# TensorE reads its moving operands from two halves in turn, with the evacuations in the matching order

## Chip, core and metric

The kernel runs on one core of a Trainium2 chip. The metric is the device time of one execution in microseconds; a run's time is the median of its executions. The profile is of one execution, taken by the hardware profiler.

## What is computed

One layer of a hybrid decoder on 512 tokens of 1,024 channels, all in float32. Cut to what matters here:

```python
h = rms_norm(x, g_mix_pre)
z = h @ w_in                                   # 1024 -> 4608: pool, rnn x, rnn gate, two merge gates
y_pool = pool_mixer(z_pool) @ w_pool_out       # causal means over 2, 4, 8, 16 tokens, small maps
y_rnn = rg_lru_branch(z_x, z_g) @ w_rg_out     # causal conv over 4 tokens, gates, linear recurrence, GELU
merged = sigmoid(z_gp) * y_pool + sigmoid(z_gr) * y_rnn
x = x + rms_norm(merged @ w_o, g_mix_post)
h = rms_norm(x, g_ffn_pre)
up = h @ w_up                                  # 1024 -> 6144
hid = gelu(causal_conv3(up[:, :3072])) * up[:, 3072:]
x = x + rms_norm(hid @ w_down, g_ffn_post)     # 3072 -> 1024
x = x + sigmoid(rms_norm(x, g_ple_gate) @ w_ple_gate) * rms_norm(p @ w_ple_proj, g_ple_post)
```

## The kernel before

Every float32 matrix is split into a high part rounded to the float32r type and a low part, the rest. A product is then three float32r matmuls into one PSUM bank, which `mm3` issues: high by high, high by low, low by high (lines 198, 199 and 200 of the profile; nearly all TensorE work carries these line numbers). ScalarE makes the high part (a copy with rounding, L412 and L193), VectorE the low one (a subtraction, `sub`, L189). Weights come from memory through `raw` tiles, and `weight(key)` keeps a few of them prepared ahead in a fixed order.

The stages, in the order in which TensorE runs them (its order is written out by hand; the other engines' order is made by a scheduler, with raised priorities where the code says `urgent`):

1. The input projection. The first four tiles (`rx`, L503) go over all channels while everything is loaded. `in_tile` makes each later tile of 128 output channels: weights stationary, the normalised transposed tokens `ht` (tag A, 512 columns) moving. `scaled` (L562) takes a tile out of its bank and multiplies it by the tokens' inverse norms `rb`. The recurrent gates (`gates`, L606) are pairs of 64-row matmuls. `pool_map`, and the two output projections into `gate` tiles (L831, L832), follow.
2. `ple_tile` projects the per-layer embedding; the product with `w_o` (`product`, tokens stationary, weight tiles `hi`, `lo` moving, 512 columns) is made by a seven-product scheme of the Strassen-Winograd kind on half blocks.
3. `add_norm` (L850, L853) and `x2_out` normalise; `h2_tile` transposes tokens on TensorE (L858) and splits them into halves of 256 tokens (`h2h`, `h2l`, tag C).
4. The up projection, also by seven products: twelve pairs of tiles, weights stationary, token forms of 256 columns moving (`products`, `up_product`; the first pair plainly by `up_plain`). Forms 5, 6, 7 and 3 are tiles of tag A that start at column 48 of their buffers (`PLACE_UP`). Forms 1, 2 and 4 lie in tag C: 1 and 2 are the first half of the tokens at column 1,072, form 4 is the second half at column 46 (`PLACE_H2`). A pair runs the products in the order 1, 3 (of the pair before), 6, 2, 7, 5, 4. `gated_half` (L998, L1000) makes the convolution along the tokens straight from the bank, `hidden` the product with the other half.
5. The down projection, seven products again, weights moving at 512 columns, then the last normalisation, `x3_tile`, and the gate of the embedding (`w_ple_gate`, 512 columns; the very last tile in two halves of 256), with its sigmoid (L164) out of PSUM and two VectorE steps before each store (L1249, L1250).

Sums of weight blocks that the schemes need are made partly on VectorE (L348) and partly by DMAs that accumulate in memory, issued from GpSimd.

The moving operand, third argument of a matmul, is a run of neighbouring columns everywhere in this version.

Of the kernel before, what the change touches and what calls it, by code (L numbers as in the profile page):

```python
# [9 lines left out]
F32 = mybir.dt.float32  # L10
F32R = mybir.dt.float32r
AF = mybir.ActivationFunctionType
# [69 lines left out]
def block_kernel(  # L82
# [79 lines left out]
    def act(o, i, func, after=None, **kw):  # L162

        ins = ACT.activation(o, i, func, **kw)  # L164
# [26 lines left out]
    def split(hi, lo, src):  # L191

        last_copy[0] = ACT.copy(hi, src)  # L193
        sub(lo, src, hi.bitcast(F32))

    def mm3(o, a, b, start, stop, **kw):
        (ah, al), (bh, bl) = a, b
        PE.matmul(o, ah, bh, start=start, stop=False, **kw)  # L198
        PE.matmul(o, ah, bl, start=False, stop=False, **kw)  # L199
        PE.matmul(o, al, bh, start=False, stop=stop, **kw)  # L200
# [17 lines left out]
    def c1(j):  # L218
        return col[:, j : j + 1]
# [277 lines left out]
    for k in range(KD):  # L497
        w = weight(("rx", k // 2), ahead=3)
        (wh, wl), (hh, hl) = w, ht(k)
        for i, (a, b) in enumerate(((wh, hh), (wl, hh), (wh, hl))):  # L500
            for m in range(4):
                o = (k % 2) * S + m * P
                PE.matmul(rx[m], a[:, o : o + P], b, start=k == 0 and i == 0, stop=k == KD - 1 and i == 2)  # L503


    bd = quad("C").rearrange("p (s a) c -> p s (a c)", s=2)
# [52 lines left out]
        return ps  # L559

    def scaled(ps, o):
        return V.tensor_tensor(o, ps, rb, ALU.mult)  # L562

    xs, xc, xcs, sig = {}, {}, {}, {}
    r_t, a_t, rg_t = {}, {}, {}
# [31 lines left out]
    def gates(cs):  # L597

        pss = {}
        for c in cs:  # L600
            pss[c] = bank(), bank()
            hi, lo = xcs[c]
            o = slice(c * P, (c + 1) * P)
            for i, (a, b) in enumerate(((0, hi), (0, lo), (1, hi))):
                for ps, pr in zip(pss[c], HEADS):
                    PE.matmul(ps, bd[pr, a, o], b[pr], start=i == 0, stop=i == 2)  # L606
        ba, bb = HEADS
        for c in cs:
            r_t[c] = slot()
            sig[c] = temp()  # L610
            g = C_BG + c
            act(r_t[c][ba], pss[c][0][ba], AF.Sigmoid, bias=col[ba, g : g + 1])
            act(sig[c][ba], pss[c][0][bb], AF.Sigmoid, bias=bias[bb, c : c + 1])
            act(r_t[c][bb], pss[c][1][ba], AF.Sigmoid, bias=bias[ba, c : c + 1])
            act(sig[c][bb], pss[c][1][bb], AF.Sigmoid, bias=col[bb, g + KD : g + KD + 1])

    def gated(c):
        inv(V.tensor_tensor(xc[c], sig[c], xc[c], ALU.mult))
# [84 lines left out]
    def pool_map(g):  # L703
        pw = weight("pool_w")
        ps = bank()
        mm3(ps, pick(pw, g * P, (g + 1) * P), pools[g], True, True)
        hi, lo = slot(F32R), slot(F32R)
        ACT.activation(hi, ps, AF.Identity, scale=c1(C_PSCALE + g))
        V.scalar_tensor_tensor(lo, ps, c1(C_PSCALE + g), hi.bitcast(F32), ALU.mult, ALU.subtract)
        yp[g] = (hi, lo)  # L710


# [25 lines left out]
    def ple_tile(t):  # L738
        pair = []
        for h in range(2):  # L740
            w = weight(("wpp", h))
            ps = bank()
            for k in range(2):
                a = pick(pq[k], t * P, (t + 1) * P)
                mm3(ps, a, pick(w, k * S, (k + 1) * S), k == 0, k == 1)
            pair.append(ps)
        outs = [slot(), slot()]
        V.tensor_copy(outs[0], pair[0])
        ACT.copy(outs[1], pair[1])
# [66 lines left out]
    for m in range(KD):  # L816
        w = weight(("wpo", m))
        pa = bank()
        for k in range(4):
            mm3(pa, pick(w, k * P, (k + 1) * P), yp[k], k == 0, k == 3)  # L820
        w = weight(("wrg", m))
        if m == KD - 1:
            o_form(1)
        split_early(1)
        pb = bank()
        for k in range(KD):
            y = yh[k // 4][:, k % 4, :], yl[k // 4][:, k % 4, :]
            mm3(pb, pick(w, k * P, (k + 1) * P), y, k == 0, k == KD - 1)
        a, b = gate[m], gate[8 + m]
        with urgent():  # L830
            V.tensor_tensor(a, pa, a, ALU.mult)  # L831
            V.tensor_tensor(b, pb, b, ALU.mult)  # L832
            V.tensor_tensor(mq[m % 2][:, m // 2, :], a, b, ALU.add)
        if m == KD - 1:
            o_form(2)
        if m == PLE_AT:
            pled = dram.tile([S, D], F32, name="pled")
            pq = []
            for k in range(2):
                raw = temp()  # L840
                nc.sync.dma_start(raw, p_t[k])
                pq.append((slot(F32R), slot(F32R)))
                split(*pq[k], raw)

    def add_norm(pair, g, res):

        og = []
        for h in range(2):
            og.append(temp())
            V.tensor_tensor(og[h], pair[h], g[h], ALU.mult)  # L850
        r = rstd_of(pair)
        for h in range(2):
            V.scalar_tensor_tensor(res[h], og[h], r, res[h], ALU.mult, ALU.add)  # L853
# [18 lines left out]
    def h2_tile(t):  # L872
        for h in range(2):
            ps = transposed(h2n[t, h]).rearrange("p (k c) -> p k c", k=4)
            hi, lo = (v[h][t // 2][:, :, t % 2 * P : (t % 2 + 1) * P] for v in (h2h, h2l))
            with tc.high_priority(offset=2 * URGENT if t else URGENT):
                split(hi, lo, ps)
                h2_done[0] = last_copy[0].ins.name
            b, c = divmod(t, 2)
            q = 10 * b + h + 11  # L880
            if c == 0:
                h2f[q] = {k: slot() for k in (0, 2)}
            for k in (0, 2):
                ACT.copy(h2f[q][k].rearrange("p (k c) -> p k c", k=2)[:, :, c * P : (c + 1) * P], ps[:, k : k + 2, :])

# [10 lines left out]
    def products(o, w, i, form, start):  # L896
        for k in range(4):
            lhs = tuple(v[:, i, k * P : (k + 1) * P] for v in w)
            rhs = tuple(v[:, k, :] for v in form)
            mm3(o, lhs, rhs, start and k == 0, k == 3, skip_group_check=True)  # L900

    def up_plain(f, b):
        for i in range(2):
# [328 lines left out]
    for h in range(2):  # L1232
        for t in range(NT):
# [5 lines left out]
            for a, b in parts:  # L1239
                ps = bank()  # L1240
                for k in range(KD):
# [3 lines left out]
                    q = (k % 4) * P  # L1245
                    x3k = pick(x3t[t, k // 4], q, q + P)
                    mm3(ps[:, a:b], x3k, pick(w, (k % 2) * S + a, (k % 2) * S + b), k == 0, k == KD - 1)
                act(o[:, a:b], ps[:, a:b], AF.Sigmoid, scale=r3[t])
                V.tensor_tensor(o[:, a:b], o[:, a:b], ple[t // 2][:, i, a:b], ALU.mult)  # L1249
                V.tensor_tensor(o[:, a:b], o[:, a:b], x3[t // 2][:, i, a:b], ALU.add)  # L1250
                nc.sync.dma_start(out[t * P : (t + 1) * P, h * S + a : h * S + b], o[:, a:b])
# [79 lines left out]
```

## Time and profile before

| | us |
|---|---|
| median of 3 runs | 735.63 (734.74 to 736.74) |
| the profiled execution, its own time | 734.33 |
| its span | 732.6 |
| TensorE busy (4,281 matmuls) | 726.2 |
| weight loads busy | 640.3 |
| VectorE busy | 577.7 |
| ScalarE busy | 443.1 |
| GpSimd busy | 82.4 |

The span is the stretch from the first to the last instruction of the profile; the 1.7 us between it and the execution's own time lie around it. A row of a group reads: line, engine, operation, result and operand by their names and shapes, count, then busy time in us, mean ns of one, and the idle time before them with what ended it. A row of the timeline begins with the start and the length in us. A row of the windows gives a stretch's length, then for each engine its busy time and count, then the granted clock, the DMA share and GB/s. Matmuls overlap and their ends are modelled, so what one costs is read from the distance between two starts.

### The profile page before, as it was taken

The numbers are of one execution on the slowest core, as the hardware profiler recorded it, in microseconds if no ns is written. First come the engines' busy times: TensorE is split into PE (matmuls) and PEld (weight loads), VectorE is DVE, ScalarE is ACT, GpSimd is POOL, SyncE is SP. The second block draws the span as 40 slices with busy tenths as digits, with TensorE's granted clock in tenths as the row PEclk, the third lists the DMA queues.
The fourth block names the chain that finished last, engine by engine and source line by source line (L and its number), as shares of the span: only waits on it lengthen the run. The fifth ranks groups of instructions, "written<-read, shape, count | busy, mean of one in ns | idle before, by whom it ended". The sixth has DMA issues, their size and how long they took to land.

```text
span 732.6 us, 11226 instructions
## 1 busy us (share of the span) xinstructions
PE 726.2 (99%) x4281; PEld 640.3 (87%) x4281; DVE 577.7 (79%) x749; ACT 443.1 (60%) x670; POOL 82.4 (11%) x107
## 2 busy tenths in 40 slices
PE   9999999999999999999999999999999999999997
PEld 7887778888888888889999999999999888888886
DVE  4896735999646668676989999998999997789852
ACT  6746779844543344577856666666667666565721
POOL 0311212100000000111013222221200000001100
PEclk9999999999999999999999999999999999999999
DMA  8999777674788987995478999898966676767011
GB/s 325 385 310 267 166 219 186 149 210 133 257 299 275 329 316 283 313 327 206 127 270 249 270 283 266 288 239 295 237 197 224 217 238 200 261 200 271 17 58 57
DMA packets 64933, 172.53 MB, mean 236 GB/s; under 512 B 5808, under 2 KB 6448, under 8 KB 64560
## 3 DMA queue, kind: packets, MB, share of 16 engines
q1 hardware_dynamic: 50336, 129.78, 51.0%
q0 software_dynamic: 14400, 41.95, 24.6%
q8 instruction: 33, 0.54, 0.3%
q14 instruction: 20, 0.16, 0.1%
q10 hardware_dynamic: 144, 0.10, 0.0%
HBM read 155.03 MB, written 58.72 MB: 292 GB/s over the span
## 4 chain that ended last, share of the span: by engine, by line
PE 96%; DMA 2%; DVE 0%; ACT 0%; SPq 0%; POOL 0%; issue 0%; DVEq 0%
PE ps L198 31%; PE ps L200 31%; PE ps L199 31%; DMA C<-in_x_dram 1%; PE ps L858 1%; PE ps L606 1%; DMA m<-in_x_t_dram 1%; PE ps L503 1%; ACT C L486 0%; SPq L403 0%; DVE lo L189 0%; POOL s L434 0%; PE ps L548 0%; DVE t L494 0%; ACT t L164 0%
## 5 line engine op out<-in xcount | busy, mean ns | idle before, releaser
L189 DVE TENSOR_TENSOR lo<-raw,hi 128x1024 fp32r<-128x1024 f32 (+2 forms) x193 | 224.7, 1184 | 53.6 <-ACT hi L412 30.6
L198 PE MATMUL ps<-A,hi 128*128 128x256 f32 (+1 forms) x608 | 197.5, 325 | 0.0
L199 PE MATMUL ps<-A,hi 128*128 128x256 f32 (+1 forms) x608 | 197.0, 324 | 0.0
L200 PE MATMUL ps<-A,lo 128*128 128x256 f32 (+1 forms) x608 | 196.9, 324 | 0.0
L412 ACT CAST hi<-raw 128x1024 fp32r<-128x1024 f32 (+1 forms) x112 | 113.0, 1015 | 110.7 <-PE ps L199 46.6
L198 PEld LDWEIGHTS ps<-A,hi 128*128 128x128 f32 x608 | 114.2, 188 | 11.2 <-issue 0.7
L200 PEld LDWEIGHTS ps<-A,lo 128*128 128x128 f32 x608 | 114.2, 188 | 10.1
L199 PEld LDWEIGHTS ps<-A,hi 128*128 128x128 f32 x608 | 114.2, 188 | 9.8
L198 PE MATMUL ps<-C,hi 128*128 128x256 f32 (+1 forms) x392 | 116.8, 298 | 0.0
L199 PE MATMUL ps<-C,hi 128*128 128x256 f32 (+1 forms) x392 | 116.4, 297 | 0.0
L200 PE MATMUL ps<-C,lo 128*128 128x256 f32 (+1 forms) x392 | 116.4, 297 | 0.0
L193 ACT CAST hi<-raw 128x1024 fp32r<-128x1024 f32 x78 | 80.7, 1052 | 31.2 <-PE ps L199 26.4
L198 PE MATMUL ps<-hi,A 128*128 128x512 f32 x224 | 87.5, 391 | 0.0
L200 PE MATMUL ps<-hi,A 128*128 128x512 f32 x224 | 87.2, 389 | 0.0
L199 PE MATMUL ps<-lo,A 128*128 128x512 f32 x224 | 87.2, 389 | 0.0
L199 PEld LDWEIGHTS ps<-C,hi 128*128 128x128 f32 x392 | 73.8, 188 | 2.6
L198 PEld LDWEIGHTS ps<-C,hi 128*128 128x128 f32 x392 | 73.7, 188 | 2.7 <-ACT rb L441 0.2
L200 PEld LDWEIGHTS ps<-C,lo 128*128 128x128 f32 x392 | 73.7, 188 | 2.5
L434 POOL TENSOR_TENSOR s<-s,mhalf 128x1 f32<-128x1 f32 (+1 forms) x21 | 15.8, 752 | 357.8 <-DVE s L447 338.7
L200 PEld LDWEIGHTS ps<-hi,A 128*128 128x128 f32 x224 | 42.1, 188 | 8.8
L198 PEld LDWEIGHTS ps<-hi,A 128*128 128x128 f32 x224 | 42.1, 188 | 8.6
L199 PEld LDWEIGHTS ps<-lo,A 128*128 128x128 f32 x224 | 42.1, 188 | 8.5
(191 smaller groups left out, 1025.6 us busy)
## 6 DMA issues: line engine op xcount, KB each, us to landing
raw<-in_w_up_dram SPq DMA_DIRECT2D x46, 512.0 KB, 6.7
wdsum<-in_w_down_dram POOLq DMA_DIRECT2D x36, 512.0 KB, 8.5
raw<-in_w_in_dram SPq DMA_DIRECT2D x32, 512.0 KB, 7.0
raw<-wdsum SPq DMA_DIRECT2D x24, 512.0 KB, 4.4
raw<-in_w_down_dram SPq DMA_DIRECT2D x18, 512.0 KB, 3.5
wosum<-in_w_o_dram POOLq DMA_DIRECT2D x12, 512.0 KB, 9.6
wdsum<-wdsum POOLq DMA_DIRECT2D x12, 512.0 KB, 7.5
parts<-hi SPq DMA_DIRECT2D x10, 512.0 KB, 4.0
```

The costliest lines, as they stand in the source:

```text
L189: V.tensor_tensor(o, a, b, ALU.subtract)
L193: last_copy[0] = ACT.copy(hi, src)
L198: PE.matmul(o, ah, bh, start=start, stop=False, **kw)
L199: PE.matmul(o, ah, bl, start=False, stop=False, **kw)
L200: PE.matmul(o, al, bh, start=False, stop=stop, **kw)
L412: ACT.copy(hi, raw)
L434: last_pow[0] = nc.gpsimd.tensor_tensor(y, v, mhalf[:, :n], ALU.pow).ins.name
L503: PE.matmul(rx[m], a[:, o : o + P], b, start=k == 0 and i == 0, stop=k == KD - 1 and i == 2)
L606: PE.matmul(ps, bd[pr, a, o], b[pr], start=i == 0, stop=i == 2)
L858: PE.transpose(ps[:, q * P : (q + 1) * P], a[:, q * P : (q + 1) * P], ident)
```

## The change

`mm3`, the first four tiles and the gates hand TensorE the moving operand through `turns`, a view of the same columns in the order 0, n/2, 1, n/2 + 1 and so on. The result's columns come out in that order, so every step that takes such a bank out of PSUM reads it through `back` (all even columns, then all odd ones) and writes its own rows plainly (`row` cuts them into the two halves). Where such a bank is squared for a norm or copied to another bank, the order is left alone.

In the up projection the tokens have to come out in order, because the convolution runs along them. There `h2_tile` stores each block of 128 tokens as its 64 even and then its 64 odd ones (`apart` reads, `kept` writes), and `near` reads a block's two halves in turn, so that the columns come out as the tokens are. The up projection's own evacuations are not changed. Transposes are not changed.

```diff
+    def turns(a):
+        return a.rearrange("p (a b) -> p b a", a=2)
+    def back(ps):
+        return ps.rearrange("p (b a) -> p a b", a=2)
+    def row(a):
+        return a.rearrange("p (a b) -> p a b", a=2)
+    def near(v):
+        return v.rearrange("p (c a b) -> p c b a", a=2, b=P // 2)
+    def apart(v):
+        return v.rearrange("p k (b a) -> p k a b", a=2)
+    def kept(v):
+        return v.rearrange("p k (a b) -> p k a b", a=2)
-    def mm3(o, a, b, start, stop, **kw):
-        (ah, al), (bh, bl) = a, b
+    def mm3(o, a, b, start, stop, order=turns, **kw):
+        (ah, al), (bh, bl) = a, map(order, b)
...
-                PE.matmul(rx[m], a[:, o : o + P], b, start=k == 0 and i == 0, stop=k == KD - 1 and i == 2)
+                PE.matmul(rx[m], a[:, o : o + P], turns(b), start=k == 0 and i == 0, stop=k == KD - 1 and i == 2)
...
     def scaled(ps, o):
-        return V.tensor_tensor(o, ps, rb, ALU.mult)
+        return V.tensor_tensor(row(o), back(ps), row(rb), ALU.mult)
...
-                    PE.matmul(ps, bd[pr, a, o], b[pr], start=i == 0, stop=i == 2)
+                    PE.matmul(ps, bd[pr, a, o], turns(b[pr]), start=i == 0, stop=i == 2)
...
-            act(r_t[c][ba], pss[c][0][ba], AF.Sigmoid, bias=col[ba, g : g + 1])
+            act(row(r_t[c][ba]), back(pss[c][0][ba]), AF.Sigmoid, bias=col[ba, g : g + 1])
...
-            V.tensor_tensor(a, pa, a, ALU.mult)
-            V.tensor_tensor(b, pb, b, ALU.mult)
+            V.tensor_tensor(row(a), back(pa), row(a), ALU.mult)
+            V.tensor_tensor(row(b), back(pb), row(b), ALU.mult)
...
-            V.tensor_tensor(og[h], pair[h], g[h], ALU.mult)
+            V.tensor_tensor(row(og[h]), back(pair[h]), row(g[h]), ALU.mult)
...
-                split(hi, lo, ps)
+                split(kept(hi), kept(lo), apart(ps))
...
-                ACT.copy(h2f[q][k].rearrange("p (k c) -> p k c", k=2)[:, :, c * P : (c + 1) * P], ps[:, k : k + 2, :])
+                ACT.copy(kept(h2f[q][k].rearrange("p (k c) -> p k c", k=2)[:, :, c * P : (c + 1) * P]), apart(ps[:, k : k + 2, :]))
...
-            mm3(o, lhs, rhs, start and k == 0, k == 3, skip_group_check=True)
+            mm3(o, lhs, rhs, start and k == 0, k == 3, near, skip_group_check=True)
...
-                act(o[:, a:b], ps[:, a:b], AF.Sigmoid, scale=r3[t])
+                act(row(o[:, a:b]), back(ps[:, a:b]), AF.Sigmoid, scale=r3[t])
```

The same `row` and `back` stand in the other three sigmoids of the gates, in `pool_map` and in the two copies of `ple_tile`.

More of the change, by code (lines that the diff above doesn't have):

```diff
@@ L611, in gates @@
             g = C_BG + c
-            act(r_t[c][ba], pss[c][0][ba], AF.Sigmoid, bias=col[ba, g : g + 1])
-            act(sig[c][ba], pss[c][0][bb], AF.Sigmoid, bias=bias[bb, c : c + 1])
-            act(r_t[c][bb], pss[c][1][ba], AF.Sigmoid, bias=bias[ba, c : c + 1])
-            act(sig[c][bb], pss[c][1][bb], AF.Sigmoid, bias=col[bb, g + KD : g + KD + 1])
+            act(row(r_t[c][ba]), back(pss[c][0][ba]), AF.Sigmoid, bias=col[ba, g : g + 1])
+            act(row(sig[c][ba]), back(pss[c][0][bb]), AF.Sigmoid, bias=bias[bb, c : c + 1])
+            act(row(r_t[c][bb]), back(pss[c][1][ba]), AF.Sigmoid, bias=bias[ba, c : c + 1])
+            act(row(sig[c][bb]), back(pss[c][1][bb]), AF.Sigmoid, bias=col[bb, g + KD : g + KD + 1])
     def gated(c):
@@ L707, in pool_map @@
         hi, lo = slot(F32R), slot(F32R)
-        ACT.activation(hi, ps, AF.Identity, scale=c1(C_PSCALE + g))
-        V.scalar_tensor_tensor(lo, ps, c1(C_PSCALE + g), hi.bitcast(F32), ALU.mult, ALU.subtract)
+        ACT.activation(row(hi), back(ps), AF.Identity, scale=c1(C_PSCALE + g))
+        V.scalar_tensor_tensor(row(lo), back(ps), c1(C_PSCALE + g), row(hi.bitcast(F32)), ALU.mult, ALU.subtract)
         yp[g] = (hi, lo)
@@ L747, in ple_tile @@
         outs = [slot(), slot()]
-        V.tensor_copy(outs[0], pair[0])
-        ACT.copy(outs[1], pair[1])
+        V.tensor_copy(row(outs[0]), back(pair[0]))
+        ACT.copy(row(outs[1]), back(pair[1]))
         s = rstd_of(pair)
```

## Prediction

> **What bounds the kernel now.** I read the page first, then the waits of TensorE, then TensorE's groups with shapes kept apart, then its timeline at chosen places, because only start times show what a matmul costs (their ends are modelled). The page:
>
> ```profile
> span 732.6 us, 11226 instructions
> PE 726.2 (99%) x4281; PEld 640.3 (87%) x4281; DVE 577.7 (79%) x749; ACT 443.1 (60%) x670; POOL 82.4 (11%) x107
> PEclk9999999999999999999999999999999999999999
> PE 96%; DMA 2%; DVE 0%; ACT 0%; SPq 0%; POOL 0%; issue 0%; DVEq 0%
> ```
>
> TensorE is busy for 99% of the span at the full granted clock, and 96% of the chain that ended last is TensorE's. All that it waited for:
>
> ```profile
> PE ps L216 <- DVE mhalf L210: 1.1, 1, 1.1
> PE ps L503 <- ACT hi L409: 0.4, 1, 0.4
> PE ps L503 <- DVE lo L189: 0.3, 1, 0.3
> ```
>
> 1.8 us, all at the start. So the time is the sum of TensorE's steps from one matmul to the next; nothing else decides anything while that stands. How many matmuls of each shape (the rows of L199 and L200 repeat those of L198 with the same counts):
>
> ```profile
> L198 PE MATMUL ps<-A,hi 128*128 128x512 f32 x256 | 100.2, 391 | 0.0
> L198 PE MATMUL ps<-A,hi 128*128 128x256 f32 x352 | 97.3, 276 | 0.0
> L198 PE MATMUL ps<-C,hi 128*128 128x256 f32 x328 | 91.9, 280 | 0.0
> L198 PE MATMUL ps<-hi,A 128*128 128x512 f32 x224 | 87.5, 391 | 0.0
> L199 PE MATMUL ps<-C,hi 128*128 128x512 f32 x64 | 24.9, 389 | 0.0
> L198 PE MATMUL ps<-hi,h 128*128 128x512 f32 x56 | 22.0, 393 | 0.0
> L503 PE MATMUL ps<-A,hi 128*128 128x512 f32 x64 | 16.5, 394 | 0.4 <-ACT hi L409 0.4
> L199 PE MATMUL ps<-m,hi 128*128 128x512 f32 x36 | 14.0, 389 | 0.0
> L503 PE MATMUL ps<-A,lo 128*128 128x512 f32 x32 | 8.7, 394 | 0.3 <-DVE lo L189 0.3
> L606 PE MATMUL ps<-m,C 64*128 64x512 f32 x48 | 6.6, 408 | 0.0
> L198 PE MATMUL ps<-hi,m 128*128 128x512 f32 x16 | 6.3, 396 | 0.0
> L198 PE MATMUL ps<-hi,h 128*128 128x256 f32 x16 | 4.5, 283 | 0.0
> L858 PE MATMUL ps<-ident,m 128*128 128x128 f32 x32 | 4.1, 272 | 0.0
> ```
>
> Three times the L198/L199 rows of 512 columns (256, 224, 64, 56, 36, 16) and the 96 of L503 are 2,052 matmuls. Of 256 columns there are 3 x (352 + 328) = 2,040 in the up product and 48 in the last gate tile. Now the steps. The first row below is a stretch of the down product by windows (470 counts two that began before it, so 468 steps up to the transpose at 671.87); the others are starts from the timeline, with what lies between two marks left out.
>
> ```profile
> 565.77:671.80 106.03, 106.03 (x470) 1.00 0.68 224
> 565.77 0.39 PE L198 MATMUL ps<-hi,A 128*128 128x512 f32 x1
> 671.87 0.27 PE L858 MATMUL ps<-ident,C 128*128 128x128 f32 x1
> ...
> 722.12 0.28 PE L198 MATMUL ps<-hi,h 128*128 128x256 f32 x1
> 727.76 0.28 PE L200 MATMUL ps<-hi,h 128*128 128x256 f32 x1
> ...
> 425.56 0.28 PE L198 MATMUL ps<-C,hi 128*128 128x256 f32 x1
> 428.44 0.28 PE L198 MATMUL ps<-C,hi 128*128 128x256 f32 x1
> 431.18 0.28 PE L198 MATMUL ps<-A,hi 128*128 128x256 f32 x1
> 436.62 0.28 PE L198 MATMUL ps<-C,hi 128*128 128x256 f32 x1
> 444.78 0.28 PE L198 MATMUL ps<-C,hi 128*128 128x256 f32 x1
> ```
>
> 512 columns: 106.10 us / 468 = 226.7 ns a step. 256 columns in the last gate tile: 5.64 / 47 = 120.0. The difference of 256 columns is 106.7 ns, so a column costs 0.417 ns and each of these matmuls loses a fixed 13.3 ns on top (226.7 - 512 x 0.417, and the same from 120.0). In the up product: 24 matmuls of product 4 from 425.56 to 428.44 step by 120.0 (loss 13.3); 48 of products 3 and 6 from 431.18 to 436.62 by 113.3 (loss 6.6). Engine, shape and weights are alike there; what differs is the column at which the moving tile starts in its buffer: 46 for product 4, 48 for 3 and 6 (PLACE_H2, PLACE_UP), and 0 for the 13.3 ns of the 512-column ones. So the loss belongs to how the moving operand is read, and the order of that reading is what this change edits.
>
> **The change part by part.** *Reading order.* Nearly every matmul reads element 0 of the first half, 0 of the second, 1 of the first and so on; columns, weights, counts and PSUM's write order stay. No row of this trace shows a moving operand read with a step, so I bound the new loss from rows. Ends: no loss left, or the old loss kept (costlier reading is a rival below). Between them lies the transpose:
>
> ```profile
> 313.85 1.03 PE L858 MATMUL ps<-ident,m 128*128 128x128 f32 x8
> ```
>
> Eight in 1.03 us of which one takes 0.272, so 7 steps of 108 ns for 128 columns, which is two columns' time each (106.7) and under 2 ns more. It is the one matmul here that changes its weights and loses next to nothing, so I take 2 ns as what is left. The reason for expecting the loss to go: the loss halves when the start moves by two columns, as a coincidence of two regular streams would; weight loads run under the matmuls all through that stage (103.00 of 103.00 us, the last row of the next fence). Read in turn, either half is passed over at half speed, so two streams that now keep step no longer do. That is argued, not shown, and costs the forecast its certainty.
>
> The sum at 2 ns left: 2,052 x 11.3 = 23.2 us; products 4 and the plain blocks of the second half of the tokens, all at column 46, (11 pairs x 24 + 96 = 360) plus 48, x 11.3 = 4.6 us; the other 1,680 x 4.6 = 7.7 us; the 48 of the recurrent gates run two at a time, 0.3 us. Together 35.8. With no loss left it would be 27.3 + 5.4 + 11.1 + 0.3 = 44.1.
>
> [...]
>
> *What takes some back.* The first 96 (L503) run while all is being loaded, and in the up product VectorE is nearly full:
>
> ```profile
> 0.00:31.00 31.00, 29.16 (x132) 23.88 (x133) 17.84 (x37) 21.29 (x32) 4.33 (x10) 1.00 0.95 359
> 31.00:100.00 69.00, 69.00 (x321) 55.35 (x319) 52.86 (x83) 42.25 (x57) 14.87 (x18) 1.00 0.92 254
> 460.00:563.00 103.00, 103.00 (x901) 103.00 (x901) 95.07 (x102) 70.17 (x111) 16.52 (x20) 1.00 0.89 248
> ```
>
> In the first stage the DMA share is 0.95, so I count nothing of its 96 x 11.3 = 1.1 us. In the third, VectorE is busy 92.3% (95.07 of 103.00). A pair of up tiles takes 444.78 - 425.56 = 19.22 us, of which VectorE needs 17.74; at 108.7 ns a step its 168 matmuls take 18.26. That leaves VectorE 0.5 us a pair, and with no loss left (17.92) 0.2. VectorE also waits for ScalarE, which waits for buffers TensorE frees, so some pairs will slip: I take 0.15 us a pair, 1.7 us in all. DMA share 0.89 there becomes 0.94: no queue gets more bytes, only less time; I charge nothing, and the same slip if it does matter. SyncE's and GpSimd's queues keep their order.
>
> *Evacuations.* They read PSUM with a step of two elements and write rows in two halves; none is added. Their durations before:
>
> ```profile
> L562 DVE TENSOR_TENSOR m<-ps,rb 128x512 f32<-128x512 f32 x16 | 11.0, 686 | 6.1 <-PE ps L200 6.1
> L193 ACT CAST C<-raw 128x1024 fp32r<-128x1024 f32 x1 | 1.0, 1045 | 0.0
> L412 ACT CAST hi<-raw 128x1024 fp32r<-128x1024 f32 x103 | 107.6, 1049 | 83.5 <-PE ps L200 34.2 <-PE ps L199 33.9 <-issue 8.5
> L164 ACT ACTIVATE t<-ps,r 128x256 f32<-128x256 f32 x2 | 0.9, 473 | 4.6 <-PE ps L200 4.6
> ```
>
> The split of the block-diagonal weights (C<-raw) walks its tile in permuted runs of 64 and takes 1,045 ns against 1,049 in plain order: a several-dimensional pattern costs nothing. A step of two within a run has no row; its ends are nothing and a doubled instruction, and I take nothing, the nearest row. Doubled, each costs some 0.7 us more on VectorE or ScalarE, hidden under TensorE (VectorE 52.86 of 69.00 us busy where most of them lie, and the up product's evacuations stay as they are, since its tokens are stored in that order). Only the last activation (473 ns, after the last matmul at 727.76) and two or three chains of normalisation lie open: at most 2 us. The token stores write the same elements in another order, eight tiles in all: nothing.
>
> So 35.8 - 1.1 - 1.7 = 33.0 us. Against the profiled execution's 734.33 us (span 732.6 and 1.7 around it) that is 701.3; its time lies 1.3 below the median of 735.63, so the median falls to 702.6.
>
> **Rivals.** *Half the loss stays:* every matmul ends at the 6.6 ns that the well-placed ones have now. Then 2,052 + 408 gain 6.7 ns, 16.5 us, the up product almost nothing, VectorE is no limit: 719. For it: 6.6 is the best this trace shows for such a matmul. Against: it takes the loss as a constant of the start, which the new order also changes.
>
> *The order doesn't matter:* the loss is in the switch of weights, the start only shifts it; then 735.6, up to 737.6 with slower evacuations. Against: the same weights and lines step by 113.3 and 120.0.
>
> *Slower, reading in turn costs time per column.* Each read now lands in another place than the one before. If a stretch that is fetched once now serves four neighbours, in turn it must be fetched anew for each. Price: at the transpose's pace, 108 / 128 = 0.84 ns a column, a 512-column step becomes 432 + 2, a 256-column one 218: 2,052 x 207 + 1,680 x 104 + 408 x 98 = 425 + 175 + 40 = 640 us, so about 1,375. It decides from 13.3 / 512 = 0.026 ns a column, 6%, on: beyond it the kernel is slower. For it: no strided moving read in the trace says otherwise. Against: each half is still a row of neighbours, so a reader that keeps two stretches open pays nothing.
>
> [...]
>
> *VectorE becomes the bound* in the up product: with no loss left there and 0.5 us a pair slipping, 735.6 - 44.1 + 1.1 + 5.5 = 698, inside the forecast's own range.
>
> **How the numbers follow.** Chances: the loss goes (forecast, with VectorE's variant) 0.47; half stays 0.14; order doesn't matter 0.14, of which 0.03 a little faster, 0.06 no change, 0.05 a little slower; time per column 0.25. A measurement of this kernel tells 0.3% from no change. So faster 0.64, same 0.06, slower 0.30. The forecast's own range is 691 (no loss left, no slip) to 711 (a quarter more of the gain missing). The range to hold 8 in 10 goes from 690 over the rivals to 750, which takes in small costs per column or at evacuations; outside lies the heavy form of the slower rival, about 0.2.
>
> **What would show it.** Steps of about 215.5 and 108.7 ns where they are 226.7, 120.0 and 113.3, the same for columns 46 and 48; TensorE still at 99% and its waits still a few us; VectorE near 97% in the up product; evacuations within a few ns of 686 and 473. Wrong if the steps are unchanged, if they grow with the number of columns, or if TensorE gets waits on VectorE or DMA worth over 5 us.

## The result, and the profile after

The changed kernel takes 712.3 us (median of 4 runs, 711.67 to 712.69) against 735.52 (734.74 to 736.74) for the kernel before beside it: a ratio of 0.9682, 95% interval 0.9665 to 0.9699. The profiled execution took 712.31 us, its span is 710.3. The page of the kernel after:

```profile
span 710.3 us, 11245 instructions
PE 699.5 (98%) x4281; PEld 637.0 (90%) x4281; DVE 576.6 (81%) x749; ACT 441.0 (62%) x670; POOL 82.3 (12%) x107
PEclk9999999999999999999999999999999999999999
PE 75%; DVE 12%; ACT 5%; DMA 3%; issue 2%; POOL 1%; SPq 0%; DVEq 0%; POOLq 0%; ACTq 0%
```

TensorE's busy time fell by 26.7 us (726.2 to 699.5), the span by 22.3. The other engines do what they did. What is new is the last row: the chain that ended last, 96% TensorE's before, now runs through VectorE and ScalarE for a sixth of the span. TensorE's waits in the kernel after (total, times, longest, in us):

```profile
PE ps L879 <- DVE h L1185: 1.7, 1, 1.7
PE ps L219 <- ACT rb L462: 1.2, 1, 1.2
PE ps L237 <- DVE mhalf L231: 1.1, 1, 1.1
PE ps L220 <- DVE m L189: 0.9, 1, 0.9
PE ps L524 <- DVE lo L189: 0.7, 1, 0.7
PE ps L219 <- ACT m L905: 0.2, 1, 0.2
PE ps L524 <- ACT A L487: 0.2, 1, 0.2
```

6.0 us where there were 1.8. The steps, from the timeline of TensorE in the kernel after; lines 219 to 221 are the former 198 to 200. What lies between two marks is left out:

```profile
412.27 0.28 PE L219 MATMUL ps<-C,hi 128*128 128x256 f32 x1
414.95 0.27 PE L219 MATMUL ps<-C,hi 128*128 128x256 f32 x1
417.63 0.28 PE L219 MATMUL ps<-A,hi 128*128 128x256 f32 x1
422.99 0.28 PE L219 MATMUL ps<-C,hi 128*128 128x256 f32 x1
431.03 0.28 PE L219 MATMUL ps<-C,hi 128*128 128x256 f32 x1
...
657.72 0.38 PE L219 MATMUL ps<-hi,A 128*128 128x512 f32 x1
665.06 0.38 PE L220 MATMUL ps<-lo,h 128*128 128x512 f32 x1
...
700.21 0.27 PE L219 MATMUL ps<-hi,h 128*128 128x256 f32 x1
705.46 0.28 PE L221 MATMUL ps<-hi,h 128*128 128x256 f32 x1
```

Product 4 (column 46): 24 steps in 2.68 us, 111.7 ns each, where it took 120.0. Products 3 and 6 (column 48): 48 in 5.36, also 111.7, where they took 113.3. The last gate tile: 47 in 5.25, 111.7. The 512-column step: 34 in 7.34 us, 215.8 ns each within the rounding of the starts, where it was 226.7. That is 512 x 0.417 + 2.5, while 111.7 is 256 x 0.417 + 5.0.

### The profile page after: what moved, and what is told of

Its sections match the earlier page's. It is cut to its first block, busy times and chain, and to the rows that moved or that the text cites. A ratio compares the mean times of both kernels' runs of the same rounds, so it can differ in the third digit from the quotient of the medians.

```text
span 710.3 us, 11245 instructions
## 1 busy us (share of the span) xinstructions
PE 699.5 (98%) x4281; PEld 637.0 (90%) x4281; DVE 576.6 (81%) x749; ACT 441.0 (62%) x670; POOL 82.3 (12%) x107
## 4 chain that ended last, share of the span: by engine, by line
PE 75%; DVE 12%; ACT 5%; DMA 3%; issue 2%; POOL 1%; SPq 0%; DVEq 0%; POOLq 0%; ACTq 0%
PE ps L219 25%; PE ps L220 25%; PE ps L221 24%; DVE lo L189 3%; ACT m L164 1%; DMA C<-in_x_dram 1%; POOL s L455 1%; DVE m L656 1%; ACT t L164 1%; ACT rb L462 1%; DVE C L189 1%; DMA m<-in_x_t_dram 1%; DVE m L947 1%; PE ps L627 1%; DVE A L1258 1%
## 5 line engine op out<-in xcount | busy, mean ns | idle before, releaser
L219 PE MATMUL ps<-A,hi 128*128 128x256 f32 (+1 forms) x608 | 194.5, 320 | 0.0
L220 PE MATMUL ps<-A,hi 128*128 128x256 f32 (+1 forms) x608 | 193.8, 319 | 0.0
L221 PE MATMUL ps<-A,lo 128*128 128x256 f32 (+1 forms) x608 | 193.8, 319 | 0.0
L219 PEld LDWEIGHTS ps<-A,hi 128*128 128x128 f32 x608 | 115.9, 191 | 8.4 <-issue 1.3
L221 PEld LDWEIGHTS ps<-A,lo 128*128 128x128 f32 x608 | 116.0, 191 | 6.9
L220 PEld LDWEIGHTS ps<-A,hi 128*128 128x128 f32 x608 | 116.0, 191 | 6.7
L219 PE MATMUL ps<-C,hi 128*128 128x256 f32 (+1 forms) x392 | 114.7, 293 | 1.5 <-ACT rb L462 1.2
L220 PE MATMUL ps<-C,hi 128*128 128x256 f32 (+1 forms) x392 | 114.3, 291 | 0.0
L221 PE MATMUL ps<-C,lo 128*128 128x256 f32 (+1 forms) x392 | 114.3, 291 | 0.0
L219 PE MATMUL ps<-hi,A 128*128 128x512 f32 x224 | 85.3, 381 | 0.0
L220 PE MATMUL ps<-lo,A 128*128 128x512 f32 x224 | 84.9, 379 | 0.0
L221 PE MATMUL ps<-hi,A 128*128 128x512 f32 x224 | 84.9, 379 | 0.0
L219 PEld LDWEIGHTS ps<-C,hi 128*128 128x128 f32 x392 | 74.7, 190 | 3.9 <-ACT rb L462 1.5
L220 PEld LDWEIGHTS ps<-C,hi 128*128 128x128 f32 x392 | 74.7, 191 | 1.8
```

## Experiments

Four questions: what makes the old loss, what in the new order takes it away, how much belongs to which part, and where the missing microseconds went. A remark for reading the rows: a matmul's mean length in a group is about 163 ns longer than its step (379 stands for 215.8, 389 for 226.7, 276 for 111.7 to 113.3, 283 for 120.0), and up to 180 ns longer at the slowest steps below; the steps in the text are taken from starts.

**Start columns (starts).** The kernel before, with other columns for the up product's forms.

```diff
-PLACES, PLACE_UP, PLACE_H2 = 64, 48, (1072, 46)
+PLACES, PLACE_UP, PLACE_H2 = 64, {5: 0, 6: 8, 7: 16, 3: 32}, (1080, 40)
-        q = quad("A", place=PLACE_UP).rearrange("p (s a) (b c) -> p s (a b) c", s=2, b=2)
+        q = quad("A", place=PLACE_UP[f]).rearrange("p (s a) (b c) -> p s (a b) c", s=2, b=2)
```

> The kernel before, with the six token forms of the up product at other start columns: product 5 at column 0, 6 at 8, 7 at 16, 3 at 32, products 1 and 2 at 1080 (56 modulo 64), product 4 at 40. Nothing else changes. Theory A (the loss is a coincidence of two regular streams, set by where the moving operand starts): steps other than 113.3 and 120.0 are possible, but they depend on the start column alone; column 0 gives 120.0 (as the 512-column tiles lose 13.3 ns there), the column 32 apart from it, 32, gives 113.3 or less if the period is 64 columns. Theory B (the loss is a matter of alignment: starts that are a multiple of 16 columns lose 6.6 ns, others 13.3): 113.3 for 0, 16 and 32, 120.0 for 8, 40 and 56. Time: products 5, 6, 7 and 3 are 1,056 matmuls in all, so up to 7 us slower.

741.28 us against 735.02 beside it (a single run of each, as for the other kernels without an interval). Column 0 steps by 118 ns in its first third and by 120.0 after it; 8, 16, 32, 40 and 1,080 (56 past a multiple of 64) step by 117 to 119. But for the 120.0 neither theory's numbers held: the loss is graded by the start, and no column tried here is as good as 48.

**Everything 64 bytes later (all64).** One more small constant ahead of all buffers.

```diff
+    V.memset(const.tile([P, 16], F32, tag="pad", name="pad"), 0.0)
```

> The kernel before with 64 bytes put ahead of all tiles, so that every moving and every stationary operand starts 16 columns later and their distance stays. Theory A1 (coincidence with the weight loads, so the distance of the two operands decides): every step as before: 226.7 for 512 columns, 113.3 and 120.0 in the up product. Theory A2 (the moving operand's own place in memory decides): the up product's 113.3 changes, to 120.0 if places repeat after 64 columns (it then lies where the last gate tile's operand lay, which had 120.0); 1,680 matmuls by 6.6 ns, 11 us slower.

735.17 us against 735.02, and every step as before (226.7, 113.3, 120.0). So the place of the moving operand alone doesn't decide.

**The weight buffers moved against the token tiles (weights192).** One pad ahead of all (192 bytes) and one in the weight pool behind the raw, high and low tiles (64). The weights move by 192 bytes and all token tiles by 256, so the distance between the two changes by 64 bytes; modulo 256 bytes only the weights move, which is how the expectation counts.

```diff
+    V.memset(const.tile([P, 48], F32, tag="pad", name="pad"), 0.0)
...
+    V.memset(wpool.tile([P, 16], F32, tag="pad2", name="pad2", bufs=1), 0.0)
```

> The kernel before with the buffers of the weights alone moved by 192 bytes (48 columns); the token forms stay. In the up product and the input tiles the stationary operand moves and the moving one stays; in the products with w_o and w_down it is the reverse. Theory A1 (distance decides): the up product's products at column 48 and 1072, which were 16 columns before the weights modulo 64, now start level with them and go from 113.3 to 120.0; the 512-column products change too, on both sides. Theory A2 (the moving operand's own place): the up product stays at 113.3 and 120.0 and the input tiles at 226.7; only the products with w_o and w_down change, to about 220, since their moving operand now starts where the up product's lucky ones do.

751.73 us against 735.02. The first fence has TensorE's groups of this kernel, the second the same group in the kernel where everything moved together:

```profile
L198 PE MATMUL ps<-A,hi 128*128 128x256 f32 x352 | 99.6, 283 | 0.0
L198 PE MATMUL ps<-hi,A 128*128 128x512 f32 x224 | 88.8, 396 | 0.0
L198 PE MATMUL ps<-hi,h 128*128 128x256 f32 x16 | 4.4, 276 | 0.0
```

```profile
L198 PE MATMUL ps<-A,hi 128*128 128x256 f32 x352 | 97.2, 276 | 0.0
```

The up product's well-placed forms went from 113.3 to 120.0 ns, the step of column 0: their distance to the weights is now a multiple of 256 bytes. The last gate tile, where the weights' buffers are the moving side, went the other way, 120.0 to 113.4 (283 to 276). Both are as the theory of the distance had it. The 512-column steps grew to 229 (input tiles) and 233.3 (w_o and down product). So the loss depends on the distance between the moving operand's address and the stationary one's; that the two reads disturb each other is the author's reading of it. It depends on the shape too: the products with w_o and w_down now have the distance at which 256 columns step by 113.3 ns, the best, and 512 columns are slower there than before.

**Other reading orders, product by product (orders).** The kernel after, with an order of its own for each product of two stages; the last gate tile is cut into 128, 128 and 256 columns.

```diff
+        ("wo", 1): blocks_of(4), ("wo", 2): blocks_of(16), ("wo", 5): blocks_of(64), ("wo", 6): blocks_of(128),
+        ("wo", 3): plain, ("wo", 7): steps_of(8), ("wo", 4): turns,
+        ("wd", 1): blocks_of(2), ("wd", 2): blocks_of(8), ("wd", 5): blocks_of(32), ("wd", 6): steps_of(2),
+        ("wd", 3): four, ("wd", 7): steps_of(4), ("wd", 4): turns,
```

`blocks_of(b)` reads the halves of each stretch of 2b columns in turn, `steps_of(n)` every nth column, then the rest, `four` the four quarters in turn.

> The changed kernel with other reading orders in the seven products with w_o and the seven with w_down (512 columns each); their banks are taken out as if the order were the old one, so these columns come out permuted. w_o: two neighbouring blocks in turn, of 4 columns in product 1, of 16 in product 2, of 64 in 5, of 128 in 6; plain in 3; every 8th column in 7; halves in 4. w_down: blocks of 2 in 1, of 8 in 2, of 32 in 5; all even then all odd columns in 6; four quarters in turn in 3; every 4th column in 7; halves in 4. The last gate tile is cut into 128, 128 and 256 columns. Theory A (an order that passes two stretches at half speed breaks the coincidence): 215.8 for blocks of 4 to 128 and for the quarters, 226.7 for plain, for blocks of 2 and for even-then-odd, which passes at double speed. Theory C (a short stretch of memory is kept open, at most two at a time): plain 226.7, blocks 215.8, but quarters, every 4th and every 8th column 400 ns or more, since each read there opens another stretch. The last tile: if what 256 columns still lose (5.0 ns against 2.5 at 512) is the loading of weights as the bound, the 128-column steps stay near 110 ns; if not, they are 56 to 58 ns.

757.9 us against 735.02. TensorE's groups in the windows of single products, in this sequence: blocks of 4 (those of 16, 64 and 128 read the same), plain, every 8th; then in the down product blocks of 2, even then odd, quarters, every 4th.

```profile
L239 PE MATMUL ps<-lo,A 128*128 128x512 f32 x8 | 3.0, 379 | 0.0
L239 PE MATMUL ps<-lo,A 128*128 128x512 f32 x8 | 3.1, 389 | 0.0
L239 PE MATMUL ps<-lo,A 128*128 128x512 f32 x8 | 4.9, 611 | 0.0
L239 PE MATMUL ps<-lo,A 128*128 128x512 f32 x24 | 9.4, 390 | 0.0
L239 PE MATMUL ps<-lo,A 128*128 128x512 f32 x24 | 15.2, 632 | 0.0
L239 PE MATMUL ps<-lo,A 128*128 128x512 f32 x24 | 10.7, 447 | 0.0
L239 PE MATMUL ps<-lo,A 128*128 128x512 f32 x24 | 15.3, 639 | 0.0
```

By starts: blocks of 4 to 128 (8 and 32 too, in the down product) step by 215.8 ns, plain by 226.7, blocks of 2 by 227, quarters by 283, every 8th by 431, even-then-odd by 453, every 4th by 460. So it isn't the distance of the halves that helps: any block from 4 columns on does. And the slower rival's price per column exists: with a step of 2, 4 or 8 a matmul takes 453, 460 and 431 ns, about twice the 226.7 of plain reading. Neither theory is left whole: A had 215.8 for the quarters and 226.7 for even-then-odd, C 400 or more for the quarters.

**Which orders cost what (orders2).** These steps sort by where the even-numbered reads alone go (the odd-numbered ones are alike). With the halves in turn, and with blocks from 4 on, they walk along four or more neighbours at a time: 215.8 ns. Plain takes them over every second column, blocks of 2 over pairs: 226.7 and 227. Even-then-odd takes them over every fourth column, the steps of 4 and 8 further: 453, 460 and 431. Quarters, 283, change the place at each of them. Five new orders in the down product ask whether this holds:

```diff
+    ORDERS = {("wd", 1): groups(2), ("wd", 2): groups(4), ("wd", 5): eighths, ("wd", 6): stepped(2), ("wd", 3): stepped(4)}
```

`groups(n)` alternates n columns of one half with n of the other; `stepped(n)` reads the halves in turn, but within them every nth column first; `eighths` takes eight parts in turn.

> The changed kernel with five more reading orders in the products with w_down (512 columns; their banks are taken out as if the order were the old one, so these columns come out permuted). Product 1: two columns of the first half, then two of the second; product 2: four and four; product 5: eight eighths in turn; product 6: the halves in turn, but all even columns of each, then all odd ones; product 3: the halves in turn with every 4th column. [...] Theory C (what counts is how many stretches are open, two at most): products 1 and 2 215.8, product 5 over 430, products 6 and 3 as the steps of two and four columns were, 450 to 460.

761.26 us against 734.78. Products 1, 2, 5, 6 and 3 in their own windows:

```profile
L231 PE MATMUL ps<-lo,A 128*128 128x512 f32 x24 | 12.1, 502 | 0.0
L231 PE MATMUL ps<-lo,A 128*128 128x512 f32 x24 | 10.0, 416 | 0.0
L231 PE MATMUL ps<-lo,A 128*128 128x512 f32 x24 | 16.0, 667 | 0.0
L231 PE MATMUL ps<-lo,A 128*128 128x512 f32 x24 | 9.3, 389 | 0.0
L231 PE MATMUL ps<-lo,A 128*128 128x512 f32 x24 | 15.2, 632 | 0.0
```

The telling one is product 6: halves in turn as in the change, but every second column within a half. Its step is 227, that of plain reading, while turns alone as the cure had 215.8 and Theory C 450 to 460. Product 3 (every fourth within a half) takes 453, product 5 487. Products 1 and 2 take 333 and 250, where Theory C had 215.8: their even-numbered reads go over every second column, as in plain reading, but also jump between the halves, and what a jump costs these runs don't give.

**Either part alone (up_plain, up_only).** The change without the up product, and only the up product of it, three rounds each.

```diff
-            mm3(o, lhs, rhs, start and k == 0, k == 3, near, skip_group_check=True)
+            mm3(o, lhs, rhs, start and k == 0, k == 3, lambda v: v, skip_group_check=True)
```

The first has `kept` and `apart` taken from `h2_tile` too. The second keeps those and `near`, and makes `turns`, `back` and `row` hand back what they get.

> The changed kernel with the up product alone put back: tokens stored in their order, moving operands of 256 columns read plainly. If every step's saving counts in full: the up steps go back to 113.3 and 120.0, 1,680 x 1.7 + 360 x 8.3 ns = 5.8 us more than the changed kernel, so about 718. If VectorE or the waits of the changed kernel hide part of it: under 716.

> The kernel before with the new order in the up product alone; everything else reads plainly and is taken out plainly. If savings add up: 5.8 us less than before, about 730, with steps of 111.7 in the up product and 226.7 elsewhere. The rest of the change is then worth 23.2 - 5.8 = 17.4 us. If the up product's saving depends on what the other stages gain (the pace of weights): clearly more or less than 5.8.

Without the up product 718.41 us, ratio 0.9769 (0.9754 to 0.9784); the up product alone 729.80, ratio 0.9924 (0.9909 to 0.9938); 734.78 for the kernel before beside them. The gains of 16.4 and 5.0 us add up to 21.4 of the whole's 23.2. Each has the new step where its order is new and the old one elsewhere. The up product holds 2,040 of the 4,281 matmuls and brings under a quarter of the gain.

**Half of the weights (half_weights).** Why 111.7 ns, and not 109.2, which is the same 2.5 ns on top that 512 columns keep? In `orders` the cut last tile had given a hint; the seventh and the sixteenth of its matmuls of 128 columns, then a group of the later ones:

```profile
743.99 0.28 PE L238 MATMUL ps<-hi,h 128*128 128x128 f32 x1
745.00 0.28 PE L238 MATMUL ps<-hi,h 128*128 128x128 f32 x1
...
L238 PE MATMUL ps<-hi,h 128*128 128x128 f32 x10 | 2.8, 275 | 0.0
```

Nine steps in 1.01 us: 112 ns for half the columns. Something that doesn't depend on the moving columns takes 111.7 ns. In the kernel after, products 7 (new order) and 2 (made plain) of the up projection and 6 (new order) and 2 (plain) of the down projection now load only 64 stationary columns; product 1 of the down projection is plain with all 128.

```diff
+            n, order = {7: (HEAD, near), 2: (HEAD, lambda v: v)}.get(f, (P, near))
+            products(o[:, a : a + HALF], w, i, forms[f], f in (1, 5), n, order)
...
+                n = HEAD if (name, f) in (("wd", 2), ("wd", 6)) else P
...
+                    (lambda v: v) if (name, f) in (("wd", 1), ("wd", 2)) else turns,
```

> The changed kernel with half of the stationary columns (64 of 128) in two products of the up projection (7 in the new order, 2 in plain order) and two of the down projection (6 in the new order, 2 in plain order), and product 1 of the down projection in plain order with all columns; half of these products' rows are left out, and the plain ones' columns come out in another order. Theory W (the loads of weights take turns from the plain reading, and bound the short matmuls): down 1 226.7, down 2 about 220, down 6 215.8 as with all columns, up 7 109.2 in place of 111.7, up 2 about 110. If the loss came from the moving operand's start alone and 111.7 were a fixed cost of a short matmul: 226.7, 226.7, 215.8, 111.7, 113.3.

714.25 us against 735.51. First the weight loads of line 220 (after the count the least, median and longest length in ns), then TensorE's groups in the windows of products 7 and 2 of one pair of up tiles:

```profile
L220 PEld LDWEIGHTS ps<-C,hi x392: 133/189/192, 208.1 to 546.3; 128*128 128x128 f32 x152, 128*64 128x64 f32 x44
...
L219 PE MATMUL ps<-A,hi 128*64 128x256 f32 x8 | 2.2, 272 | 0.0
L219 PE MATMUL ps<-C,hi 128*64 128x256 f32 x8 | 2.2, 281 | 0.0
```

Product 7 steps by 109.2 ns: with half of the weights the extra 2.5 ns are gone. The loads agree: 64 columns fewer shorten one by some 56 ns (189 to 133), 0.87 ns a column, so 128 take an estimated 112. The up product's step in the new order, 111.7 ns, is thus that of its weight loads. Products 6 and 1 of the down projection step by 215.8 and 226.7 ns, as expected. The plain products refuted the second half of the expectation: 118.5 to 119 and 230.0 ns where 110 and 220 were expected. The loss of the plain order isn't in proportion to the weights read.

**Taking the new waits away (smooth, pool_later, smooth2).** The kernel after has three long waits of TensorE that the kernel before doesn't have (1.7, 1.2 and 0.9 us). `smooth` moves the order written out by hand: each gate tile before the pool map, the up projection's first product of pair 1 behind the third token tile's transposes, the last token tile into a gate tile of the first half.

```diff
-O_AFTER = (("up", 11), ("up", 21), ("tr", 2), ("up", 12), ("up", 22), ("tr", 3), ("p1", 1))
+O_AFTER = (("up", 11), ("up", 21), ("tr", 2), ("p1", 1), ("up", 12), ("up", 22), ("tr", 3))
...
-    IN_ORDER += [("map", _g), ("gate", 8 + _g)]
+    IN_ORDER += [("gate", 8 + _g), ("map", _g)]
...
+                    if (h, t, k) == (0, 2, 4):
+                        x3_tile(3)
...
-            if (h, t) == (0, 1):
-                x3_tile(3)
```

> The changed kernel with TensorE's written order mended at the three places where it now waits: each pool map comes after the gate tile that followed it; the first product of pair 1 comes before the plain products 12 and 22; the last token tile's transposes come inside the next gate tile. If these waits are what the missing gain went into (1.2 + 1.3 + 1.7 us): 4 us less than the changed kernel, about 708, and the steps unchanged. If the wait only moves to the next tile of the same chain: no change, 712.

713.53 us, ratio 0.9692 (0.9669 to 0.9716), not 708. The wait of the pool map went, the one on `rb` stayed, and that of the last token tile moved into the gate tile behind it. TensorE's waits there, and its timeline just behind the first of them:

```profile
PE ps L219 <- ACT h L193: 1.8, 1, 1.8
PE ps L219 <- ACT rb L462: 1.3, 1, 1.3
...
674.82 0.63 PE L219 MATMUL ps<-hi,h 128*128 128x512 f32 x1
675.24 0.63 PE L220 MATMUL ps<-lo,h 128*128 128x512 f32 x1
```

Behind that wait and another of 0.5 us six matmuls step by 427 ns (0.42 here), twice 213, which costs 1.3 us more; the mean granted clock of this execution is 0.997, and 1.000 in that of the kernel after. TensorE's order was thus the wrong lever: the chain on the other engines was late whatever TensorE did in the meantime. What it waited for stood on VectorE in the kernel after:

```profile
667.58 1.40 POOL L455 TENSOR_TENSOR s<-s,mhalf 128x1 f32<-128x1 f32 x1 [6.50 <-DVE s L468]
669.00 0.16 DVE L1188 COPY r<-s 128x1 f32<-128x1 f32 x1 [0.44 <-POOL s L455]
669.08 1.22 DVE L189 TENSOR_TENSOR lo<-raw,hi 128x1024 fp32r<-128x1024 f32 x1
670.21 0.15 DVE L468 SCALAR_TENSOR_TENSOR s<-s,s 128x1 f32<-128x1 f32 x1
```

The 0.15 us that begin the last normalisation (L468) stand behind a copy that waits for GpSimd and behind 1.22 us of weight splitting, which TensorE needs only later. `pool_later` has only the second of the edits above. `smooth2` has it too, and clears VectorE's queue at those places: ScalarE takes both banks of the embedding's projection, the inverse norms are written where they are needed and not copied, and the low parts of the gate weights' second half stand behind the last normalisation.

```diff
-        V.tensor_copy(row(outs[0]), back(pair[0]))
+        ACT.copy(row(outs[0]), back(pair[0]))
...
-        V.tensor_copy(rp[t], s)
+        rstd_of(pair, rp[t])
...
-        V.tensor_copy(r3[t], s3)
+        rstd_of(res, r3[t])
...
+            if key[0] == "wpg" and key[2] == 1:
+                behind(low, normed[0])
```

> The changed kernel with one thing more: each pool map comes after the gate tile that followed it, so VectorE has another 5 us to split the pooled rows. If the wait at the first pool map (1.2 us) is simply TensorE come too early: 1.2 us less than the changed kernel, about 711.1, every other stretch as it was.

> pool_later, and the two other long waits taken at the chains that end late and not in TensorE's order: ScalarE takes out both banks of the embedding's projection (VectorE took one, queued behind a normalisation that waits for GpSimd); the inverse norms are written where they are used, without a copy on VectorE that waits for GpSimd; the low parts of the last gate's second half of weights come after the last normalisation on VectorE, not before it. If VectorE's queue is what makes these chains late: 1.3 and 1.7 us less than pool_later, about 708, and the gaps before the second plain block of the up product and before the last token tile shrink to under 0.5 us. If the chains themselves are too long: no less than 710.

Five rounds on one chip, the kernel before at 735.69. `pool_later`: 711.51 us, ratio 0.9674 (0.9661 to 0.9688), not to be told from the change's 0.9682. Its wait is gone, but about 1.0 us of it comes back at 272 us, in the product with w_o, as two short waits for ScalarE and VectorE. `smooth2`: 707.92 us, ratio 0.9626 (0.9609 to 0.9643), the best of all. Its waits:

```profile
PE ps L237 <- DVE mhalf L231: 1.1, 1, 1.1
PE ps L526 <- DVE lo L435: 0.7, 1, 0.7
PE ps L221 <- DVE h L189: 0.6, 1, 0.6
PE ps L526 <- ACT A L489: 0.6, 2, 0.4
PE ps L526 <- ACT hi L430: 0.2, 1, 0.2
```

3.2 us, all but 0.6 of them in the loading stage. The three long new ones are gone; the 0.6 is what is left of the last token tile's, a little over the 0.5 expected. Of the 5.2 us between the spans of `smooth2` and the kernel after, 0.6 lie in the loading stage, which these edits leave alone.

## Why the prediction was right, and where it wasn't

**The forecast case came true**, with the size of its gain too large: the old loss goes with the reading order, and TensorE's steps carry the time. The median is 712.3 us where 702.6 was predicted, the profiled execution 712.31 where the sum gave 701.3. Of these 11.0 us the steps account for 6.9 and the waits and restarts for 5.5, less the 1.7 us set aside for VectorE; 0.3 is left over. The result lies inside the wide range (690 to 750) but just outside the forecast's own (691 to 711). And its sign of being wrong, waits of TensorE on VectorE or DMA over 5 us, was nearly met: those on VectorE are 4.4 us, with ScalarE's 6.0.

**The 512-column term held.** 215.8 ns against 215.5 taken from the transposes: without the first four tiles 1,956 x 10.9 = 21.3 us, where the prediction had 23.2 - 1.1 = 22.1. The closeness is partly luck: the transposes are no yardstick for these matmuls. They too step by 109 ns with 128 stationary columns, but their loads last 141 ns in the kernel before, and those of the others 188. That the first four tiles would bring nothing was right. Here are the windows' first row, and the one of the up product, for the kernel after:

```profile
0.00:31.00 31.00, 29.03 (x128) 24.83 (x129) 17.00 (x36) 20.60 (x31) 4.33 (x10) 1.00 0.94 356
443.00:541.00 98.00, 98.00 (x880) 98.00 (x879) 92.67 (x100) 65.45 (x106) 17.46 (x22) 1.00 0.93 260
```

At 31 us TensorE has done 128 matmuls, 132 before. The DMA share is 0.94, and TensorE waits there for 2.0 us, 1.1 of them on `mhalf` and 0.9 on tiles made from what is loaded. It also started slower: its first 20 matmuls took 4.6 us in place of 3.8, because in this execution 18 and not 11 of them stepped at half pace (213 ns).

**The mis-sized term is that of the 256-column matmuls.** The step that failed is "I take 2 ns as what is left", carried over from the transposes to every shape. It gives 108.7 ns; 111.7 was measured. The 7.7 and 4.6 us for them became 1,680 x 1.67 = 2.8 and 408 x 8.33 = 3.4. Together with the gates' 0.35 the steps bring 27.8 us in place of 35.8 - 1.1 = 34.7. The runs show what the transposes couldn't: in these float32r matmuls the loading of 128 stationary columns holds the step at 111.7 to 112 ns. Three measurements agree on it: 128 moving columns step by 112 as well, 64 stationary ones give 109.2, and a load's length grows by 0.87 ns a column. That columns 46 and 48 would step alike was right.

**VectorE's slip of 0.15 us a pair did not occur.** In the second row above, the up product's: TensorE 98.00 of 98.00, VectorE 92.67 (94.6%). A pair takes 431.03 - 412.27 = 18.76 us, its 168 x 111.7. Slower steps than forecast left VectorE more room. That the 1.7 us set aside for it cover a part of the waits that came elsewhere is luck.

**Waits came elsewhere, which the prediction did not have.** "Its waits still a few us" was meant as 1.8; they are 6.0. Of the 27.8 us the span shows 22.3. 4.2 of the difference of 5.5 are the added waits: the first pool map (0.9), the token sums `rb` before the second half's plain block (1.2), the last token tile (1.7), and small ones. About 0.4 us of the difference, 0.2 of it waits, are in the first stage; the rest of about 1 us I read as restarts behind the waits, not shown one by one. The chains of the long ones run through VectorE, ScalarE and GpSimd, whose instructions stand in the same order and last as long as before. With TensorE's long matmuls 5% quicker they are no longer in time. `smooth2` shows it for two of them by shortening the chains.

**Evacuations cost nothing**, as taken. The two groups in the kernel after, 686 and 473 ns before:

```profile
L583 DVE TENSOR_TENSOR m<-ps,rb 128x512 f32<-128x512 f32 x16 | 10.9, 684 | 0.0
L164 ACT ACTIVATE t<-ps,r 128x256 f32<-128x256 f32 x2 | 0.9, 474 | 4.1 <-PE ps L221 4.1
```

**The reason was half right.** The prediction argued a coincidence of two streams, the moving read and the weight loads. That the distance between the two operands' addresses matters is shown by `weights192` (113.3 to 120.0 ns, and 120.0 to 113.4 in the last gate tile). But putting the two out of step is not what helps: product 6 of `orders2` reads the halves in turn as well and steps by 227 ns. What the runs show goes with the even-numbered reads alone. Over every second column a matmul takes 226.7 ns for 512 columns and, read from column 48, 113.3 for 256, both 0.443 ns a column; over every fourth 453, 0.885 a column, twice as much. Halved again, for neighbours, it would be 0.221, less than the 0.417 that a column costs, so by the author's estimate the columns (512 x 0.417 = 213.3) set the time there; 215.8 was measured. The slower plain steps lie up to some 6.7 ns above this pace: 120.0 for 256 columns, and 233.3 for 512 in `weights192`. So the fixed 13.3 ns that the prediction saw at both lengths may be two things, one that goes with the order and one with the distance. What is shown is that the loss is the same at both lengths only at the one distance (0, modulo 256 bytes): at the other 256 columns lose 6.6 ns and 512 lose 20.0. The rest is an estimate that fits most runs, not shown: with half of the weights the plain steps grew, to 118.5 to 119 and 230.0, and the 333 and 250 of `groups` have no place in it.

**The slower rival** had a price that exists, but not in the order that the change takes. Even-then-odd, every 4th, every 8th, eighths, and halves by every fourth column paid 431 to 487 ns, close to its 432; the halves in turn take 215.8. Its "four neighbours" came out too, in blocks of columns: those of 4 step by 215.8, those of 2 by 227. Its supposition, that in turn a stretch must be fetched anew for each column, had 432 for them.

**The other rivals.** "The order doesn't matter" and VectorE as the bound are out by the steps and by 94.6%. "Half the loss stays" is out at 512 columns (2.5 of 13.3 ns left), but came near at 256, where 5.0 ns are left against its 6.6, by another cause: with 64 stationary columns 2.5 ns are left there too (109.2), with all 128 the weight load sets the step (111.7).

## What to carry to other kernels

A gain per instruction that is read off one shape holds for another only if no second limit lies between: ask for each shape what else takes about as long, here the weight load of an estimated 112 ns beside a 109 ns matmul. In this kernel, with weight loads running beside the float32r matmuls, a moving operand read from two halves in turn, or in turn from blocks of 4 columns and more, took 5% off the 512-column ones (226.7 to 215.8 ns), and the matching read of the bank was free (686 and 684 ns, 473 and 474). When the busiest engine gets quicker, look for chains on the others that were just in time: they took back a fifth of the gain, and shortening VectorE's queue ahead of them brought most of it back, where moving TensorE's work alone did not.

## What the runs showed of the hardware that was not expected

- The step depends on the address distance between the moving and the stationary operand: in `weights192`, moving the two by 64 bytes against each other turned 113.3 into 120.0 ns (256 columns) and 226.7 into 233.3 (512); in `all64`, moving both by 64 changed nothing.
- The order of the columns changes a 512-column step (`orders`, `orders2`): 215.8 ns where the even- and the odd-numbered reads each walk along neighbours, four or more at a time; 226.7 to 227 where they take every second column, 453 every fourth, quarters 283, eighths 487.
- A load of 128 stationary float32r columns takes an estimated 112 ns of its own (0.87 a column in `half_weights`), and the float32r matmuls of 256 columns step by 111.7 with it, by 109.2 with 64 stationary columns.
- Behind waits of 1.8 and 0.5 us in `smooth` six matmuls of 512 columns ran at half pace (427 ns); what slowed them is not shown.
